# An encoder block on one core: the last mixer tile by column halves, the router spread over the tiles, rows stored unmodulated

## The chip, the core and the metric

The kernel runs on one NeuronCore of a Trainium2 chip. The metric is the device time of one execution in microseconds (us). The engines are TensorE (PE, matrix products and transposes), VectorE (DVE), ScalarE (ACT), GpSimd (POOL) and SyncE (SP, here only an issuer of transfers). Each engine works through its own list of instructions in order; lists meet through semaphores.

## What is computed

One layer of an encoder on 1024 positions of 1024 channels, in float32: a conditioning vector gives shifts, scales and gates; a mixer (Fourier branch and short convolution, gated) adds to the residual; then 16 experts with expert choice, and a last norm. The part around the change:

```python
x = x + gate_m[:, None, :] * mix_out              # mix_out = z @ w_o

h2 = modulate(rms_norm(x, g_norm_moe[l]), shift_f, scale_f)   # h*(1+scale)+shift
# expert_choice_moe(h2):
probs = softmax(h2 @ w_router + b_router)          # 16 experts
vals, idx = top_k(probs of each expert over positions, 128)
a = xe @ w_gate_e ; u = xe @ w_up_e                # xe: the 128 rows chosen
y = (silu(a) * u) @ w_down_e * vals
x = x + gate_f[:, None, :] * scatter_add(y at idx)
return rms_norm(x, g_final)
```

Products are made in three passes: each operand is split into a high part (rounded) and a low part (the rest), and high x high, high x low and low x high are summed.

## The kernel before

A planner of the language orders each engine's instructions when the kernel is built: what stands earlier in the program goes first, as soon as the planner believes its inputs and buffers ready. `tc.issue_after(ins)` holds instructions back behind another one. So a pool's number of buffers also moves the order.

*Mixer output, `mix_out` (L726).* Eight tiles t of 128 positions. A tile makes z @ w_o as 48 matmuls into one two-bank PSUM tile, for each k both column halves (`mm3`, L99). Then DVE adds the halves to x (L814, tile `ld`), ACT squares and sums them (L819), POOL makes the reciprocal root (`rstd`, L658), and DVE modulates the row in four pieces (L828, L830) into `h`, which POOL's queue stores to `h2_d` (L831); x itself goes to `x2_d` (L821). Modulation needs two rows broadcast to all partitions, loaded at t = 0. The router of tile t-1 stands at k = 6 of tile t: eight transposes with their split (`turn`, L731), 16 small matmuls against router weights that hold the modulation (`logits`, L743), softmax, and then `compare` (L848) for experts 0 and 1. Tile 7 has nobody behind it: its turning, router and the ranking of tiles 6 and 7 follow its last matmul.

*Ranking.* Experts 0 and 1 are ranked by counting, tile after tile (`compare`: how many earlier values are at least as large, by a matmul against ones; the own tile's row by a transpose), so that expert 0 can be picked right behind tile 7. The other experts are ranked by a bisection in small steps (`router`, L894), handed out between the weight blocks of the first experts through `side`.

*Picking, `pick` (L961).* A one-hot over the place, matmuls against position and probability, an index, and an indirect gather of 128 normed rows from `h2_d` into `xg` on POOL's queue. `turn` (L994) transposes them in two halves into PSUM and splits them into `xh` and `xl`.

*Experts, `expert` (L1048).* The weights come as 24 units of 1 MB per expert through a ring of slots, issued by SP in the order of use (`fetch`, L1006), 15 slots in three pools (7 + 5 + 3). `unit` (L1023) splits a unit in two halves: ACT writes the rounded part (`whi`, L92 in `split`), DVE the rest (`wlo`, L93); each has 3 buffers. A half feeds six matmuls. For each quarter fc of the 2048 hidden channels there are a gate block (`a`), an up block (`u`), and down blocks into `y`, which lag one quarter. Before the last down block of expert e the rows of expert e+1 are turned. Behind it DVE weighs y by probability and gate (`ys`, L1126), and POOL adds it into `x2_d` by an indirect transfer (L1127). In the last expert the finished rows of `x2_d` come back as four extra units in the weight stream (places in `FIN`), are normed by `final` (L1159: two sums of squares and a scaling on ACT, a product on DVE, one on POOL) and stored; the last expert's own 128 rows follow.

## Time and profile before

| | |
|---|---|
| median of 3 runs | 1964.37 us (1959.64 to 1964.53) |
| profiled execution | 1961.4 us, span 1959.6 us |
| PE busy | 1881.2 us (96%), 8677 matmuls and transposes |
| VectorE busy | 1608.2 us (82%) |
| ScalarE busy | 1169.2 us (60%) |
| mean granted PE clock | 0.984 |
| moved by DMA | 549.03 MB, mean 280 GB/s |
| chain that ended last | PE 79%, DVE 10%, issue 6%, ACT 2% |

The mixer output begins near 640 us, the experts near 783 us, and the last expert's matmuls end near 1947 us. Busy shares are means over stages with different limits. Matmuls are pipelined and their ends are modelled, so a full PE may still hold short gaps. In a row of the chain or of a timeline the first two numbers are start and duration in us, and the bracket gives the idle time before the instruction and who ended it. The granted clock is given as a share of full speed.

### The profile page before, as it was taken

Reading aid. Unit: us, or ns where it says so; the run is one execution under the profiler, and the core shown is the slowest. Engines: PE = TensorE matmul, PEld = TensorE weight load, DVE = VectorE, ACT = ScalarE, POOL = GpSimd, SP = SyncE. Lnnn points to the kernel's source line nnn. Section 1 sums busy time; section 2 is a strip of 40 time slices with the busy share of each in tenths; the row PEclk is TensorE's granted clock in tenths of the full one; section 3 lists DMA queues with packets and bytes.
Section 4 is the critical chain, followed back from the end, with each engine's and each line's share of the span. In section 5 each row is a group of like instructions: output and inputs, shape, how many; then the busy total and the mean of one; then the engine's idle time right before and its main releaser. Section 6 shows DMA issues by size and latency. Waiting matters only on the chain.

```text
span 1959.6 us, 24141 instructions
## 1 busy us (share of the span) xinstructions
PE 1881.2 (96%) x8677; PEld 1505.6 (77%) x8677; DVE 1608.2 (82%) x2083; ACT 1169.2 (60%) x1402; POOL 141.7 (7%) x127
## 2 busy tenths in 40 slices
PE   6999999999999996999999999999999999999985
PEld 5788888777788874777888888777777877777764
DVE  5976669676753777999999999899999899998985
ACT  5533233433411422777777777777777777777784
POOL 1000000000131111000000000000000000000011
PEclk9999999999999997999999999999999999999997
DMA  8322224464764945999999999999999999999981
GB/s 296 128 65 65 86 86 151 160 223 171 258 240 121 328 148 208 361 327 375 373 369 384 376 370 356 384 363 356 387 359 360 381 365 361 381 369 350 378 309 79
DMA packets 245261, 549.03 MB, mean 280 GB/s; under 512 B 12644, under 2 KB 51652, under 8 KB 245140
## 3 DMA queue, kind: packets, MB, share of 16 engines
q1 hardware_dynamic: 230160, 496.07, 70.0%
q0 software_dynamic: 14128, 51.18, 8.2%
q8 instruction: 68, 1.11, 0.2%
q14 instruction: 53, 0.43, 0.1%
q10 hardware_dynamic: 852, 0.24, 0.1%
HBM read 507.61 MB, written 39.86 MB: 279 GB/s over the span
## 4 chain that ended last, share of the span: by engine, by line
PE 79%; DVE 10%; issue 6%; ACT 2%; DMA 1%; POOL 1%; POOLq 0%; SPq 0%; ACTq 0%; DVEq 0%
PE pb L314 9%; PE u L1157 6%; PE pa L314 6%; DVE wlo L93 6%; PE pc L314 6%; PE u L1155 6%; PE u L1156 6%; PE a L1157 5%; PE a L1156 4%; PE a L1155 4%; PE y L105 4%; PE y L108 4%; PE y L111 4%; PE mm L111 3%; PE mm L105 3%
## 5 line engine op out<-in xcount | busy, mean ns | idle before, releaser
L93 DVE TENSOR_TENSOR wlo<-raw,whi 128x1024 fp32r<-128x1024 f32 x765 | 912.1, 1225 | 64.9 <-ACT whi L92 52.4
L92 ACT ACTIVATE whi<-raw 128x1024 fp32r<-128x1024 f32 x765 | 803.1, 1060 | 216.0 <-PE y L111 78.1
L1157 PE MATMUL a<-wlo,xh 128*128 128x512 f32 x512 | 208.5, 407 | 10.3 <-DVE wlo L93 9.5
L1155 PE MATMUL a<-whi,xh 128*128 128x512 f32 x512 | 204.4, 399 | 6.8 <-ACT whi L92 6.8
L1157 PE MATMUL u<-wlo,xh 128*128 128x512 f32 x512 | 204.7, 400 | 2.4 <-DVE wlo L93 1.8
L1155 PE MATMUL u<-whi,xh 128*128 128x512 f32 x512 | 204.3, 399 | 0.2 <-ACT whi L92 0.2
L1156 PE MATMUL a<-whi,xl 128*128 128x512 f32 x512 | 203.4, 397 | 0.2 <-DVE xl L93 0.2
L1156 PE MATMUL u<-whi,xl 128*128 128x512 f32 x512 | 202.7, 396 | 0.0
L108 PE MATMUL y<-wlo,hth 128*128 128x512 f32 x508 | 162.6, 401 | 2.6 <-DVE wlo L93 2.6
L105 PE MATMUL y<-whi,hth 128*128 128x512 f32 x508 | 160.8, 397 | 2.4 <-ACT whi L92 2.4
L111 PE MATMUL y<-whi,htl 128*128 128x512 f32 x508 | 158.6, 393 | 0.0
L1157 PEld LDWEIGHTS a<-wlo,xh 128*128 128x128 f32 x512 | 97.0, 190 | 44.5 <-DVE wlo L93 23.3
L92 ACT ACTIVATE wh<-s 128x512 fp32r<-128x512 f32 x80 | 50.3, 631 | 134.9 <-PE pc L314 73.4
L1157 PEld LDWEIGHTS u<-wlo,xh 128*128 128x128 f32 x512 | 96.7, 189 | 28.9 <-DVE wlo L93 6.1
L1155 PEld LDWEIGHTS a<-whi,xh 128*128 128x128 f32 x512 | 97.5, 190 | 27.1 <-ACT whi L92 7.2
L1156 PEld LDWEIGHTS a<-whi,xl 128*128 128x128 f32 x512 | 97.4, 190 | 23.4 <-DVE xl L93 0.7
L1156 PEld LDWEIGHTS u<-whi,xl 128*128 128x128 f32 x512 | 96.7, 189 | 21.9
L1155 PEld LDWEIGHTS u<-whi,xh 128*128 128x128 f32 x512 | 96.8, 189 | 21.0 <-ACT whi L92 0.6
L111 PEld LDWEIGHTS y<-whi,htl 128*128 128x128 f32 x508 | 95.8, 189 | 21.0
L105 PEld LDWEIGHTS y<-whi,hth 128*128 128x128 f32 x508 | 93.8, 189 | 22.0 <-ACT whi L92 2.9
L108 PEld LDWEIGHTS y<-wlo,hth 128*128 128x128 f32 x508 | 92.0, 189 | 22.0 <-DVE wlo L93 4.5
L92 ACT ACTIVATE wh<-ld 128x512 fp32r<-128x512 f32 x68 | 42.4, 629 | 88.1 <-issue 36.1
(523 smaller groups left out, 3157.2 us busy)
## 6 DMA issues: line engine op xcount, KB each, us to landing
raw<-in_w_gate_e_dram SPq DMA_DIRECT2D x128, 1024.0 KB, 8.4
raw<-in_w_up_e_dram SPq DMA_DIRECT2D x126, 1024.0 KB, 7.6
raw<-in_w_down_e_dram SPq DMA_DIRECT2D x126, 1024.0 KB, 8.2
ld<-in_w_ada_dram SPq DMA_DIRECT2D x48, 512.0 KB, 5.0
ld<-in_w_in_dram SPq DMA_DIRECT2D x44, 512.0 KB, 4.6
sg_d<-q POOLq DMA_DIRECT2D x8, 1024.0 KB, 5.0
ld<-sg_d SPq DMA_DIRECT2D x16, 512.0 KB, 4.3
x<-in_x_dram SPq DMA_DIRECT2D x8, 512.0 KB, 5.1
```

Source lines behind the costliest of these rows:

```text
L92: self.nc.scalar.activation(hi, src, AF.Copy)
L93: self.nc.vector.tensor_tensor(lo, src, hi, op=OP.subtract)
L105: nc.tensor.matmul(o, lhsT=lh, rhs=rh, start=first, stop=False)
L108: nc.tensor.matmul(o, lhsT=lh, rhs=rl, start=False, stop=False)
L111: nc.tensor.matmul(o, lhsT=ll, rhs=rh, start=False, stop=last)
L314: nc.tensor.matmul(o, lhsT=x[:, k, :], rhs=y[:, k, :], start=first and k == 0 and i == 0, stop=last and k == 3 and i == 2, skip_group_chec ...
L1155: nc.tensor.matmul(o, lhsT=lhs[0], rhs=rhs[0], start=first, stop=False)
L1156: nc.tensor.matmul(o, lhsT=lhs[1], rhs=rhs[0], start=False, stop=False)
L1157: nc.tensor.matmul(o, lhsT=lhs[0], rhs=rhs[1], start=False, stop=last)
```

## The change

It has five parts, all in the second half of the kernel.

1. Tile 7 is made by column halves: first all k for columns 0 to 511, then for 512 to 1023. Add, square sum, turning and router matmuls of the first half run while the second half is made.
2. The router of the tile before is spread: the ranking of the tile before that at k = 0, turning at k = 2, router matmuls and softmax at k = 4 (in tile 7 at k = 0, 4 of the first and 0 of the second half). `compare` takes both experts together, in two parts around a `yield`, makes the own row first, copies it on ACT, and counts ties with one more compare over the own tile. The softmax is made on negated logits, which saves the subtraction of the maximum.
3. Rows are stored normed but unmodulated, one ACT copy with the row's factor in place of four DVE pieces, and in tile 7 on SP's queue, ahead of the store of x. The modulation is made in the experts' `turn`, where channels lie on partitions: for expert 0 four ACT and four DVE pieces of 128x128 per half, for the others four ACT pieces per half into an f32 buffer `xf`, a copy and a subtraction. The column vectors `vc` stay in memory for it.
4. The weighing of y and its scatter-add are put off behind the first weight unit of the next expert (`self.left`, run in `up`); the load of the final gain follows them.
5. The ring shrinks from 7 + 5 + 3 to 7 + 4 + 1 slots, the split buffers grow from 3 to 6 of each part. How many halves are split ahead of the first gather (`NWS` in `unit`) stays 3.

```diff
-NRA, NRB, NRC, NWO = 7, 5, 3, 6
-NWS = 3
+NRA, NRB, NRC, NWO = 7, 4, 1, 6
+NWS, NWB = 3, 6
...
+        def turn(x2, xt, hf):
+
+            xth, xtl, pt = xt
+            hs = slice(4 * hf, 4 * hf + 4)
+            for k in range(4 * hf, 4 * hf + 4):
+                nc.tensor.transpose(pt[:, k, :], x2[:, k * P:(k + 1) * P], self.ident)
+            self.split(xth[:, hs, :], xtl[:, hs, :], pt[:, hs, :])
...
+        def softmax(t, rs, pl):
...
+            nc.vector.tensor_reduce(mn, lg, axis=AX.X, op=OP.min)
             se = pool.tile([P, 1], F32, name="se", bufs=2)
-            nc.scalar.activation(lg, lg, AF.Exp, accum_out=se)
+            nc.scalar.activation(lg, lg, AF.Exp, scale=-1.0, bias=mn, accum_out=se)
             nc.vector.reciprocal(se, se)
             nc.vector.tensor_scalar(self.prob[:, t, :], lg, se, None, op0=OP.mult)
...
+        def psum():
+            return self.pss.tile([P, 512], F32, name="sm")
+
+        def add_x(x2, ps, i):
+            cs = slice(512 * i, 512 * i + 512)
+            nc.vector.tensor_tensor(x2[:, cs], ps[:, cs], x2[:, cs], op=OP.add)
+
+        def sumsq(x2, h2, ss, i):
+            cs = slice(512 * i, 512 * i + 512)
+            nc.scalar.activation(h2[:, cs], x2[:, cs], AF.Square, accum_out=ss[:, i:i + 1])
+
+        def norm(x2, h2, ss, ts, eng):
+            nc.vector.tensor_tensor(ss[:, 0:1], ss[:, 0:1], ss[:, 1:2], op=OP.add)
+            rs = self.rstd(pool, ss[:, 0:1], "y")
+            nc.scalar.activation(h2, x2, AF.Copy, scale=rs)
+            eng.dma_start(out=self.h2_d[ts, :], in_=h2)
+            self.afterld = eng.dma_start(out=self.x2_d[ts, :], in_=x2).ins
+            return rs
+
+        def side(n):
+
+            if prev is None:
+                return
+            t, x2, rs = prev
+            if n == 0 and t:
+                for _ in self.compare(t - 1, range(NCMP), psum):
+                    pass
+            if n == 2:
+                hold["xt"] = turned()
+                for hf in range(2):
+                    turn(x2, hold["xt"], hf)
+            if n == 4:
+                pl = psum()
+                for hf in range(2):
+                    logits(pl, hold["xt"], hf)
+                softmax(t, rs, pl)
+
+        prev, hold = None, {}
...
+            if t < ST - 1:
+                for k in range(KD):
+                    side(k)
+                    self.mm3([ps[:, 0:512], ps[:, 512:1024]], (zh[:, k, :], zl[:, k, :]),
+                             [(self.wo[0][:, k, n:n + 512], self.wo[1][:, k, n:n + 512]) for n in (0, 512)],
+                             first=(k == 0), last=(k == KD - 1))
+                for i in range(2):
+                    add_x(x2, ps, i)
+                for i in range(2):
+                    sumsq(x2, h2, ss, i)
+                prev = (t, x2, norm(x2, h2, ss, ts, nc.gpsimd))
+                continue
+            xt = None
+            for n in range(2):
+                cs = slice(512 * n, 512 * n + 512)
+                for k in range(KD):
+                    if n == 0 and k % 2 == 0:
+                        side(k // 2)
+                    if n == 1 and k == 0:
+                        side(4)
+                    if n == 1 and k == 3:
+                        xt = turned()
+                        turn(x2, xt, 0)
+                    if n == 1 and k == 5:
+                        cmp = self.compare(t - 1, range(NCMP), psum)
+                        next(cmp)
+                    if n == 1 and k == 7:
+                        pl = psum()
+                        logits(pl, xt, 0)
+                    self.mm3([ps[:, cs]], (zh[:, k, :], zl[:, k, :]), [(self.wo[0][:, k, cs], self.wo[1][:, k, cs])],
+                             first=(k == 0), last=(k == KD - 1))
+                add_x(x2, ps, n)
+                if n == 0:
+                    sumsq(x2, h2, ss, n)
+            next(cmp, None)
+            turn(x2, xt, 1)
+            sumsq(x2, h2, ss, 1)
+            rs = norm(x2, h2, ss, ts, nc.sync)
+            logits(pl, xt, 1)
+            softmax(t, rs, pl)
...
+        for i in range(ne):
+            nc.tensor.transpose(row[:, i, :], p[i].to_broadcast([P, P]), self.ident)
+        if not last:
+            nc.scalar.activation(self.prow[:, e0:e0 + ne, n:n + P], row, AF.Copy)
+        ms = []
+        for i, e in enumerate(es):
+            w = n if last else n + P
+            m = pool.tile([P, (ST - 1) * P], BF16, name="cmp", bufs=2)
+            nc.vector.tensor_scalar(m[:, 0:w], self.prow[:, e, 0:w], p[i], 0.0, op0=OP.is_ge, op1=OP.add,
+                                    accum_out=cnt[:, 0, i:i + 1])
+            ms.append(m)
+        for i, e in enumerate(es):
+            own = pool.tile([P, P], BF16, name="own", bufs=2)
+            r = row[:, i, :] if last else self.prow[:, e, n:n + P]
+            nc.vector.scalar_tensor_tensor(own, in0=r, scalar=p[i], in1=self.upper, op0=OP.is_equal, op1=OP.mult,
+                                           accum_out=cnt[:, 1, i:i + 1])
+            if last:
+                own = pool.tile([P, P], BF16, name="own", bufs=2)
+                nc.vector.tensor_scalar(own, r, p[i], 0.0, op0=OP.is_ge, op1=OP.add, accum_out=cnt[:, 2, i:i + 1])
+        yield
+        for i in range(ne):
+            for j in range(t):
+                nc.tensor.matmul(num[:, i, j:j + 1], lhsT=ms[i][:, j * P:(j + 1) * P], rhs=self.onesb[:, 0:1],
+                                 start=True, stop=True)
...
+            nc.vector.tensor_tensor(place[:, :, 0:t], place[:, :, 0:t], num[:, :, 0:t], op=OP.subtract)
+        own = place[:, :, t]
+        if last:
+            nc.vector.tensor_tensor(cnt[:, 0, :], cnt[:, 0, :], cnt[:, 2, :], op=OP.add)
+        nc.vector.tensor_tensor(cnt[:, 0, :], cnt[:, 0, :], cnt[:, 1, :], op=OP.subtract)
+        self.after = nc.vector.tensor_tensor(own, own, cnt[:, 0, :], op=OP.add).ins
...
-        nc.vector.tensor_tensor(oh, self.pos[:, :, e:e + 1].to_broadcast([P, ST, P]),
+        pos = self.place[:, e, :, None] if e < NCMP else self.pos[:, :, e:e + 1]
...
+    def turn(self, pool, idx, val, xg, first=False):
...
+            hs = slice(4 * hf, 4 * hf + 4)
+            f = pool.tile([P, 4, P], F32, name="xf")
+            for k in range(4):
+                a, b = (self.vc[:, j + 4 * hf + k:j + 4 * hf + k + 1] for j in (16, 0))
+                if first:
+                    nc.scalar.activation(xh[:, 4 * hf + k, :], pt[:, k, :], AF.Identity, scale=a, bias=b)
+                    nc.vector.tensor_scalar(f[:, k, :], pt[:, k, :], a, b, op0=OP.mult, op1=OP.add)
+                else:
+                    nc.scalar.activation(f[:, k, :], pt[:, k, :], AF.Identity, scale=a, bias=b)
+            if not first:
+                nc.scalar.activation(xh[:, hs, :], f, AF.Copy)
+            nc.vector.tensor_tensor(xl[:, hs, :], f, xh[:, hs, :], op=OP.subtract)
...
                         self.mm3x(ps, (xh[:, k, :], xl[:, k, :]), (wh[:, i, :], wl[:, i, :]), k == 0, k == KD - 1)
                         k += 1
+                if self.left:
+                    self.left.pop()()
...
+            if last and fc == 0:
+                self.gl = pool.tile([P, D], F32, name="ys")
+                nc.gpsimd.dma_start(out=self.gl, in_=self.io["g_final"].rearrange("(o d) -> o d", o=1)
+                                    .partition_broadcast(P))
...
         if not last:
             down(3, 1)
-            ys = pool.tile([P, D], F32, name="ys")
-            nc.vector.scalar_tensor_tensor(ys, in0=y, scalar=val, in1=self.gf, op0=OP.mult, op1=OP.mult)
-            nc.gpsimd.indirect_dma_start(out=self.x2_d, out_offset=bass.IndirectOffsetOnAxis(ap=idx[:, 0:1], axis=0),
-                                         in_=ys, in_offset=None, compute_op=OP.add)
-            self.scattered = e == NE - 2
+
+            def add():
+                ys = pool.tile([P, D], F32, name="ys")
+                nc.vector.scalar_tensor_tensor(ys, in0=y, scalar=val, in1=self.gf, op0=OP.mult, op1=OP.mult)
+                nc.gpsimd.indirect_dma_start(out=self.x2_d,
+                                             out_offset=bass.IndirectOffsetOnAxis(ap=idx[:, 0:1], axis=0),
+                                             in_=ys, in_offset=None, compute_op=OP.add)
+                self.scattered = e == NE - 2
+
+            self.left.append(add)
...
-        gwsp, self.wsp = pool("mwsp", "right", bufs=NWS)
+        gwsp, self.wsp = pool("mwsp", "right", bufs=NWB)
...
+        picked = self.turn(mp, *picked, first=True)
+        self.left = []
```

## Rows read from the trace of the kernel before

**Rows 1.** Busy time by stretch (columns first): handover, middle experts, last expert.

```profile
core 0: us, PE busy (x) PEld busy (x) DVE busy (x) ACT busy (x) POOL busy (x), PEclk, DMA share, GB/s
700.00:740.00 40.00, 39.57 (x224) 31.77 (x223) 28.82 (x109) 9.34 (x21) 3.87 (x7) 1.00 0.24 92
...
760.00:780.00 20.00, 5.59 (x46) 4.83 (x46) 15.64 (x59) 2.20 (x4) 4.97 (x6) 0.50 0.82 307
...
1004.86:1074.90 70.04, 69.86 (x322) 56.61 (x321) 65.91 (x64) 55.31 (x58) 3.87 (x2) 1.00 1.03 375
1357.22:1428.61 71.39, 70.55 (x322) 56.23 (x320) 64.66 (x64) 55.05 (x59) 3.62 (x3) 1.00 1.01 367
1900.00:1930.00 30.00, 19.87 (x71) 14.59 (x70) 20.52 (x19) 22.07 (x29) 9.20 (x6) 0.77 0.30 120
```

**Rows 2.** Chain that ended last, from the last mixer tile on: start, us, what.

```profile
753.79 0.70 DVE ld L814
...
755.92 0.69 DVE htl L93
...
767.90 6.65 DMA h_d<-h
...
775.59 4.95 DMA xg<-h_d,idx
...
783.70 0.80 PE a L1156
```

**Rows 3.** Timeline of DVE, router and pick of the last tile.

```profile
765.11 0.23 DVE L752 SCALAR_TENSOR_TENSOR lg<-sm,yrs,rb 128x16 f32<-128x16 f32 x1 [1.91 <-PE sm L749]
...
768.59 1.15 DVE L859 TENSOR_SCALAR_CACHE_REDUCE cmp<-prow,prob 128x896 bf16<-128x896 f32 x1
...
771.84 1.22 DVE L968 TENSOR_TENSOR oh<-pos,slot 128x1024 bf16<-128x1024 f32 x1
...
773.72 0.16 DVE L981 SCALAR_TENSOR_TENSOR idx<-r 128x1 int32<-128x1 f32 x1
```

**Rows 4.** Timeline of PE: first and last of tile 7's 16 router matmuls.

```profile
761.51 0.37 PE L747 MATMUL sm<-wr,hth 128*128 128x32 f32 x1
...
764.71 0.36 PE L749 MATMUL sm<-wr,htl 128*128 128x16 f32 x1
```

**Rows 5.** Groups by line and shape, 640 to 785 us.

```profile
L830 DVE TENSOR_TENSOR h<-h,sf 128x512 f32<-128x512 f32 x16 | 10.9, 684 | 0.0
...
L92 ACT ACTIVATE zh<-ya 128x128 fp32r<-128x128 f32 x4 | 1.0, 298 | 5.0 <-DVE ya L610 5.0
L93 DVE TENSOR_TENSOR zl<-ya,zh 128x128 fp32r<-128x128 f32 x4 | 1.0, 278 | 0.0
```

**Rows 6.** Groups of ACT, whole run: eviction without and with scale and shift.

```profile
L92 ACT ACTIVATE hth<-tp 128x512 fp32r<-128x512 f32 x64 | 37.5, 586 | 8.9 <-PE tp L1077 8.2
...
L218 ACT ACTIVATE hg<-sm,shift,scale 128x512 f32<-128x512 f32 x4 | 3.0, 772 | 4.3 <-PE sm L142 4.3
```

**Rows 7.** Tile xg: its 17 gathers, issue to landing.

```profile
DMA to landing us min/median/max: 3.4/7.9/9.7
```

**Rows 8.** Timeline of POOL: two of 15 scatter-adds, seven experts apart.

```profile
1285.91 2.32 POOL L1127 DMA_INDIRECT x_d<-ys,idx  x1 [48.98 <-DVE ys L1126]
...
1785.31 2.32 POOL L1127 DMA_INDIRECT x_d<-ys,idx  x1 [51.58 <-DVE ys L1126]
```

**Rows 9.** Timeline of PE just after an expert begins.

```profile
1786.22 0.51 PE L1157 MATMUL a<-wlo,xh 128*128 128x512 f32 x1 [0.66 <-DVE wlo L93]
```

**Rows 10.** Waits of PE, 740 to 1960 us: total, times, longest.

```profile
PE a L1157 <- DVE wlo L93: 9.5, 16, 1.4
```

**Rows 11.** Timeline of PE, last expert: first and last of five stops.

```profile
1910.56 0.79 PE L1155 MATMUL a<-whi,xh 128*128 128x512 f32 x1 [6.76 <-ACT whi L92]
...
1937.69 1.22 PE L108 MATMUL y<-wlo,hth 128*128 128x512 f32 x2 [1.84 <-DVE wlo L93]
```

**Rows 12.** Waits of SP, 780 to 1900 us: total, times, longest.

```profile
SPq L1018 <- DVE wlo L93: 876.9, 342, 24.8
```

More of the change, by code (lines that the diff above doesn't have):

```diff
@@ L801, in mix_out @@
             ps = self.psm.tile([P, D], F32, name="mm")
-            for k in range(KD):
-                if k == 6 and prev is not None:
-                    logits(t - 1, prev[1], *turn(prev[0]))
-                    for e in range(NCMP):
-                        self.compare(self.cmpp, lambda: self.pss.tile([P, 512], F32, name="sm"), t - 1, e)
-                self.mm3([ps[:, 0:512], ps[:, 512:1024]], (zh[:, k, :], zl[:, k, :]),
-                         [(self.wo[0][:, k, n:n + 512], self.wo[1][:, k, n:n + 512]) for n in (0, 512)],
-                         first=(k == 0), last=(k == KD - 1))
@@ L810, in mix_out @@
             h2 = pool.tile([P, D], F32, name="h2")
             ss = pool.tile([P, 2], F32, name="ss2", bufs=2)
-            for i in range(2):
-                cs = slice(512 * i, 512 * i + 512)
-                nc.vector.tensor_tensor(x2[:, cs], ps[:, cs], x2[:, cs], op=OP.add)
-            if t == ST - 1:
-                xt = turn(x2)
-            for i in range(2):
-                cs = slice(512 * i, 512 * i + 512)
-                nc.scalar.activation(h2[:, cs], x2[:, cs], AF.Square, accum_out=ss[:, i:i + 1])
@@ L841, in router_consts @@
         nc.vector.tensor_copy(self.v5[:, :, :, 0:2], tk[:, :, None, :].to_broadcast([P, ST, NE, 2]))
+        self.vc = pool.tile([P, 24], F32, name="vc")
         self.prow = pool.tile([P, NCMP, (ST - 1) * P], F32, name="prow")
@@ L846, in router_consts, with compare @@
                                     op0=OP.mult, op1=OP.add)
-    def compare(self, pool, psum, t, e):
+    def compare(self, t, es, psum):
         nc = self.nc
-        p = self.prob[:, t, e:e + 1]
-        place = self.place[:, e, :]
+        pool = self.cmpp
+        e0, ne = es[0], len(es)
+        place = self.place[:, e0:e0 + ne, :]
         n = t * P
-        cnt = pool.tile([P, 3], F32, name="cnt", bufs=2)
+        last = t == ST - 1
+        cnt = pool.tile([P, 3, ne], F32, name=f"cnt{ne}", bufs=2)
@@ L856, in compare @@
         pc = psum()
-        if t:
-            m = pool.tile([P, (ST - 1) * P], BF16, name="cmp", bufs=2)
-            nc.vector.tensor_scalar(m[:, 0:n], self.prow[:, e, 0:n], p, 0.0, op0=OP.is_ge, op1=OP.add,
-                                    accum_out=cnt[:, 0:1])
-            for i in range(t):
-                nc.tensor.matmul(pc[:, P + i:P + i + 1], lhsT=m[:, i * P:(i + 1) * P], rhs=self.onesb[:, 0:1],
-                                 start=True, stop=True)
-        nc.tensor.transpose(pc[:, 0:P], p.to_broadcast([P, P]), self.ident)
@@ L865, in compare @@
-        if t < ST - 1:
-            row = self.prow[:, e, n:n + P]
-            nc.vector.tensor_copy(row, pc[:, 0:P])
-        else:
-            row = pc[:, 0:P]
-        own = pool.tile([P, P], BF16, name="own", bufs=2)
-        nc.vector.scalar_tensor_tensor(own, in0=row, scalar=p, in1=self.low, op0=OP.is_equal, op1=OP.mult,
-                                       accum_out=cnt[:, 1:2])
-        nc.vector.tensor_scalar(own, row, p, 0.0, op0=OP.is_gt, op1=OP.add, accum_out=cnt[:, 2:3])
-        if t:
-            nc.vector.tensor_tensor(place[:, 0:t], place[:, 0:t], pc[:, P:P + t], op=OP.subtract)
-            nc.vector.tensor_tensor(place[:, t:t + 1], place[:, t:t + 1], cnt[:, 0:1], op=OP.add)
@@ L877, in compare @@
-        nc.vector.tensor_tensor(place[:, t:t + 1], place[:, t:t + 1], cnt[:, 1:2], op=OP.add)
-        last = nc.vector.tensor_tensor(place[:, t:t + 1], place[:, t:t + 1], cnt[:, 2:3], op=OP.add)
-        if t == ST - 1:
-            self.after = last.ins
-            nc.vector.tensor_copy(self.pos[:, :, e], place)
+        row = pc[:, 0:ne * P].rearrange("p (e s) -> p e s", e=ne)
+        num = pc[:, 256:256 + 8 * ne].rearrange("p (e t) -> p e t", e=ne)
+        p = [self.prob[:, t, e:e + 1] for e in es]
@@ L956, in route_rest @@
     def route_rest(self, pool):
-        self.compare(self.cmpp, self.psum, ST - 1, 1)
+        yield from self.compare(ST - 1, (1,), self.psum)
         self.ranked = NCMP
@@ L1283, in run @@
         nc.gpsimd.dma_start(out=self.trib, in_=self.seg("tri"))
-        for n in ("slot", "tok", "low"):
+        for n in ("slot", "tok", "upper"):
             a, b = SEG[n]
@@ L1312, in psum @@
             return self.ptp.tile([P, 512], F32, name="tp")
-        self.compare(p, psum, ST - 1, 0)
+        for _ in self.compare(ST - 1, (0,), psum):
+            pass
         with tc.issue_after(self.after):
```

106 lines of the change are left out of this document (36 added, 70 removed).

## The prediction

> **What bounds the kernel now.** I read the busy time by stretch first, then the chain that ended last through the handover from mixer to experts, then the timelines of single engines where that chain stops, and last the waits.
>
> By stretch, TensorE (PE) is the bound almost everywhere: 39.57 of 40.00 us busy while mixer tiles run, 69.86 of 70.04 us in an expert [rows 1]. VectorE stands right behind it in an expert (65.91 us), ScalarE has room (55.31 us). The DMA share of 1.0 looks like a second bound, but SP, which issues the weight loads, spent 876.9 us in 342 waits for the split that frees a ring slot [rows 12]: the loads wait for the engines. So three places are left where PE loses time.
>
> The handover: between 760 and 780 us PE is busy 5.59 of 20 us, at half clock [rows 1]. The chain [rows 2] starts with the add of the last mixer tile at 753.79, goes through router, ranking, the storing of the normed rows (landed 6.65 us after 767.90) and the gather (4.95 us from 775.59), and reaches the second matmul of expert 0 at 783.70: 29.9 us.
>
> The expert boundary: a period is 70.04 us in a good expert and 71.39 us in most later ones [rows 1]; seven of the latter take 499.4 us, 71.34 each [rows 8]. Right behind the boundary PE waits for a low part of a weight split on VectorE [rows 9], 16 times, 9.5 us [rows 10]; the y weighing and the two row splits are queued there among the weight splits.
>
> The last expert: PE stops five times, 6.76, 1.36, 1.84, 2.44 and 1.84 us, 14.2 in all, the first and the last of them in [rows 11], for splits queued behind the final norm of rows. From 1900 to 1930 its clock is 0.77 [rows 1], so by that share some 3 to 5 us more (an estimate) go to the lower of its two levels.
>
> **The change part by part.**
>
> *Handover.* From the end of the last matmul of tile 7, the new chain is: add of one half and its turning. Before, add to second split piece took 755.92 + 0.69 - 753.79 = 2.8 us [rows 2]; I keep it. Router matmuls of one half only, the other half having run inside the tile: 16 took 764.71 - 761.51 + 0.4 = 3.6 us [rows 4], so 8 take 1.8. Softmax: 768.59 - 765.11 = 3.5 us [rows 3], of which three modulation pieces of 0.68 to 0.74 us [rows 5] stood in between; without them 1.4. Ranking against the earlier tiles: 771.84 - 768.59 = 3.25 [rows 3]; the wide compare (1.15) and both own-tile counts stay, the transposed row now comes first and the copy of the places goes: 2.7. One-hot, matmuls, index: 773.72 + 0.16 - 771.84 = 2.0. Issue of the gather 0.5. Its landing was 4.95 us, the median of all 17 is 7.9, the slowest 9.7 [rows 7]; now it falls into the four weight loads issued just before it, so I take 6.4, between the first two. Turning of expert 0's rows to its matmul: 783.70 - 775.59 - 4.95 = 3.2, plus four pieces of 0.278 [rows 5] on VectorE for the modulation: 4.3. Sum 2.8 + 1.8 + 1.4 + 2.7 + 2.0 + 0.5 + 6.4 + 4.3 = 21.9 against 29.9, 8.0 less. The storing of the normed rows is off the chain: sum of squares, power and one copy on ScalarE (twice 0.586 us [rows 6]) put its issue some 4 us after the add, and with the 6.65 us of before it lands at 11, about when the index is ready (11.2); were it 3 us later, all 3 would be lost. To be paid: tile 7 now holds eight router matmuls (0.9 warm), the rest of tile 6's, four transposes and its ranking, about 2 us of PE ahead of the end; the earlier tiles can return at most the 0.43 us of idle per 40 us [rows 1], 1 us. Handover: 7 us gained, bounds 3 (slowest gather) and 10.
>
> *Spreading the router steps over a tile* costs and gives nothing else: PE runs the same matmuls and was busy. VectorE drops the modulation, four pieces of 0.7 us per tile; ScalarE gets one copy of 1.2 us per tile, covered by its idle time (9.34 of 40 us busy [rows 1]). Fewer loads at tile 0 are hidden by the stream.
>
> *Expert boundary.* The weighing of y moves behind the first weight unit of the next expert, and the split buffers grow from 3 to 6 pairs. One pair feeds PE for 69.86 / 48 = 1.46 us, so PE has 4.4 us more in hand. If every period became the good one, seven give 1.3 each, 9; with the boundaries before and behind them I put it at 11. Against it stands the modulation in each turn. ScalarE evicts 128x512 in 0.586 us, with scale and shift in 0.772 [rows 6], 0.19 more; a 128x128 piece takes 0.298 [rows 5], so with both about 0.48. Eight of these and two copies are 5.0 us where 1.2 were, 3.9 more in each of 15 turns. ScalarE's total goes to 59 of 70 us, which it has; the added time in the turn must be covered by split pairs in hand. I take 8 us gained, bounds 14 gained (also the short waits of good boundaries gone) and 15 lost (1 us at each boundary).
>
> The Trainium skill (ScalarE: Activation LUTs, Rules for kernel authors) speaks against this part: multiplies and adds belong on VectorE. Its figures (same page, What ACT_TABLE_LOAD costs) put a 128-column piece with two pointer operands at 0.48 us, overlapping by 0.09; by that the turn costs 3.1 us more, not 3.9, and the sum stays. On the rule itself the row decides otherwise: VectorE is 94% busy in an expert and ScalarE 79% [rows 1], so the eight pieces would hurt more there.
>
> *Last expert.* The stops come where ScalarE is in the final norms of rows, two of them in a row, and the splits behind them wait. Three more pairs hide 4.4 us of the first stop; the later ones find the buffers refilled only in part. 5 us gained, bounds 0 (norms drawn together differently) and 14.
>
> *Ring of 12 slots, not 15.* 12 MB at 375 GB/s [rows 1] are 33 us of stream; loads wait for slots today, so nothing. Cover gone would mean splits waiting for loads, which no wait shows now. *Scatter-add one unit (2 x 1.46 = 2.9 us) later:* POOL waits for it anyway; behind it only the load of the final gain and the reload of rows in the last expert, which are used near its end. Nothing.
>
> Sum: 7 + 8 + 5 = 20. The profiled execution took 1961.4 us (span 1959.6), so 1941.4; the median of the runs shown is 3.0 above it, so 1944 in its terms.
>
> **The rivals.**
>
> *Everything hides.* The deeper buffers take the boundaries to their best (14) and most of the last expert (12), handover 9: 35 gained, 1929. For it: all waits behind the boundary name one queue. Against: VectorE has only 4 us per expert to run ahead with.
>
> *Only the handover.* The longer turn takes back what the buffers give, the norms stay: 7 to 9 gained, 1956. For it: with one f32 buffer for the modulated half, the second half of a turn waits for VectorE's subtraction of the first.
>
> *Slower: the turn becomes the new wait at each boundary.* Place: that f32 buffer. Chain: four pieces 1.9, copy 0.6, subtraction 0.7, twice, is 6.4 us, and PE's cover from the transposes to the second half's first use is four pairs, 5.8 us. If one weight split stands ahead on each engine in each half (1.1 and 1.2 us), the chain is 11 and PE stops 5.2 us 15 times: 78 lost less the 1.4 of today each, 57 net, less 12 from the other parts: 2009. It decides against the change from 12 / 15 = 0.8 us of stop beyond today's. Against: the turn's pieces come earlier in the program than the splits they'd wait for, and rows are gathered long ahead. By the rule of the Trainium skill given above (ScalarE: Activation LUTs, Rules for kernel authors) this would be the outcome of putting the pieces on ScalarE. Its 21% of idle time in an expert [rows 1] speaks against it.
>
> *The spread does nothing.* That PE was 99% busy through the tiles makes this nearly certain for tiles 0 to 6, and it is in the sum.
>
> **How the numbers follow.** Forecast 0.55, everything hides 0.17, only the handover 0.18, slower 0.10, most of this near the point of decision (1960 to 1985). The range 1926 to 1963 holds the first three with their bounds and leaves out the far ends. A measurement of this kernel tells 0.3% (6 us) from no change. Faster by more: 0.55 + 0.17 + 0.12 of the third and a little of the rest, 0.85; within it 0.08; slower 0.07.
>
> **What would show it.** Right: the first expert matmul about 21 us behind the last mixer add; the store of normed rows landed before the gather's index; 15 even periods below 70.8 us, no wait of PE for a low part behind a boundary; in the last expert the first stop near 2 us. Wrong: PE waiting for a row split (xh or xl) after each turn; splits waiting for weight loads; the gather waiting for the store; stops in the last expert as long as before.

## The result and the profile after

The changed kernel took 1991.94 us (median of 4 runs, 1990.36 to 1997.72) against 1963.5 of the kernel before in the same comparison: ratio 1.0154, 95% interval 1.0128 to 1.0179. It is slower by 28 us, where I had forecast 20 faster.

By stretch (the changed kernel; span, busy time per engine, granted clock):

```profile
640.00:660.00 20.00, 17.16 (x82) 13.68 (x82) 14.23 (x25) 8.52 (x18) 2.22 (x4) 1.00 0.82 272
...
785.00:795.00 10.00, 7.16 (x28) 5.11 (x27) 8.14 (x26) 4.10 (x8) 0.00 (x0) 0.57 0.67 258
1012.58:1084.06 71.48, 70.52 (x322) 56.48 (x321) 65.94 (x64) 57.88 (x68) 3.89 (x3) 1.00 1.01 367
1446.90:1520.21 73.31, 71.53 (x320) 56.12 (x320) 64.10 (x64) 54.26 (x67) 3.63 (x3) 1.00 1.00 359
```

The last two lines are an early and a late expert, like the two in [rows 1]: where an early one took 70.04 it takes 71.48, and where a late one took 71.39 it takes 73.31, with full clock and VectorE and ScalarE no busier than 92%. The other two lines are new losses, at the start of the mixer tiles and behind the handover.

Between the start of the first mixer-output matmul, the last one, the first gate matmul of expert 1, that of expert 15 and the end of the span, the two profiled executions differ like this (from the trace's start times, us):

| stretch | before | after | difference |
|---|---|---|---|
| eight mixer tiles | 113.5 | 121.9 | +8.3 |
| last mixer matmul to expert 1 | 105.0 | 102.9 | -2.1 |
| experts 1 to 14 | 995.7 | 1017.7 | +22.1 |
| expert 15 and the end | 105.6 | 105.9 | +0.4 |

So the experts lost 22, a mean of 1.58 in each of 14 periods: 5.4 in experts 2 to 5, 17.0 in experts 6 to 14, while expert 1 gave 0.3 back. The handover gained too little to pay for the tiles. With 0.2 from before the tiles the sum is, within rounding, the 29.0 between the spans 1959.6 and 1988.6.

**The late boundary** (the ten into experts 6 to 15). ScalarE between two late experts of the changed kernel:

```profile
1433.86 0.60 ACT L92 ACTIVATE hth<-tp 128x512 fp32r<-128x512 f32 x1 [1.60 <-PE tp L1151]
1434.35 2.00 ACT L92 ACTIVATE whi<-raw 128x1024 fp32r<-128x1024 f32 x2
1438.47 1.51 ACT L1072 ACTIVATE xf<-tp,vc 128x128 f32<-128x128 f32 x4 [2.12 <-PE tp L1063]
1439.86 1.07 ACT L92 ACTIVATE whi<-raw 128x1024 fp32r<-128x1024 f32 x1
1440.81 0.64 ACT L1074 ACTIVATE xh<-xf 128x512 fp32r<-128x512 f32 x1
...
1444.60 1.09 ACT L92 ACTIVATE whi<-raw 128x1024 fp32r<-128x1024 f32 x1
```

VectorE and PE there:

```profile
1436.17 2.35 DVE L93 TENSOR_TENSOR wlo<-raw,whi 128x1024 fp32r<-128x1024 f32 x2
1440.96 1.23 DVE L93 TENSOR_TENSOR wlo<-raw,whi 128x1024 fp32r<-128x1024 f32 x1 [2.44 <-ACT whi L92]
...
1445.34 1.28 DVE L1202 SCALAR_TENSOR_TENSOR ys<-y,val,gf 128x1024 f32<-128x1024 f32 x1 [0.28 <-PE y L111]
1446.54 1.22 DVE L93 TENSOR_TENSOR wlo<-raw,whi 128x1024 fp32r<-128x1024 f32 x1
```

```profile
1442.24 0.74 PE L108 MATMUL y<-wlo,hth 128*128 128x512 f32 x2 [0.53 <-DVE wlo L93]
1447.81 0.50 PE L1236 MATMUL a<-wlo,xh 128*128 128x512 f32 x1 [1.03 <-DVE wlo L93]
```

ScalarE splits two halves, and then its next instruction is the first modulation piece, whose transposes PE has not made yet. It sits idle for 2.12 us with buffers free, then does 1.51 us of pieces before the next split. VectorE starves for 2.44 us, and PE comes to the missing low part at 1442.24. The second stop (1.03 at 1447.81) ends with the low part of 1446.54. Its high part was ready at 1445.69, behind the second four pieces. By then VectorE stood at the weighing of y (part 4), which waited 0.28 for PE and ran until 1446.62. So both the pieces and the weighing stand ahead of that split, and no run separates what each costs here.

**The early boundary** (the four into experts 2 to 5) is another case. There ScalarE does not stop for the transposes. The second half's pieces wait for VectorE to empty the one f32 buffer `xf`, and PE waits for the rows' low part `xl`. Waits between 800 and 1900 us (who waited for whom, us in total, times, longest):

```profile
PE a L1235 <- DVE xl L1075: 2.7, 4, 0.9
ACT xf L1072 <- DVE xl L1075: 2.0, 4, 0.7
```

**The tiles.** In tile 1 PE sums the router weights' products; a row of PE's timeline, and one of VectorE's with what that sum waits for:

```profile
658.37 1.93 PE L786 MATMUL sm<-wsf,ones 128*128 128x16 f32 x16 [2.76 <-DVE wsf L779]
```

```profile
657.64 0.18 DVE L775 COPY vc<-sm 128x24 f32<-128x24 f32 x1 [2.87 <-DMA z_d<-ya]
```

The first write of the channel vectors `vc` waits for a store of `ya`, a block of the merge stage that has nothing to do with them. Tile 1 took 20.3 us where it had taken 13.4, and the clock granted between 660 and 680 was 0.91.

**The handover**, in the chain of waits:

```profile
762.99 0.61 DVE ld L795
...
773.15 0.67 issue
773.81 8.49 DMA xg<-h_d,idx
782.44 1.10 PE tp L1063 x4
...
789.46 0.80 PE a L1235
```

From the add to the second matmul it is 26.5 us against 29.9 [rows 2].

### The profile page after: what moved, and what is told of

It reads as the page before. It is cut to its first block, busy times and chain, and to the rows that moved or that the text cites. A ratio compares the mean times of both kernels' runs of the same rounds, so it can differ in the third digit from the quotient of the medians.

```text
span 1988.6 us, 23938 instructions
## 1 busy us (share of the span) xinstructions
PE 1897.5 (95%) x8677; PEld 1505.4 (76%) x8677; DVE 1575.3 (79%) x1978; ACT 1184.8 (60%) x1543; POOL 144.3 (7%) x124
## 4 chain that ended last, share of the span: by engine, by line
PE 79%; DVE 9%; issue 4%; DMA 4%; ACT 3%; POOL 1%; ACTq 0%; POOLq 0%; DVEq 0%
PE pb L314 8%; PE pa L314 6%; PE pc L314 6%; PE u L1236 5%; PE y L108 5%; DVE wlo L93 5%; PE y L105 5%; PE u L1235 5%; PE y L111 5%; PE u L1234 5%; PE a L1236 4%; PE a L1235 4%; PE a L1234 4%; PE mm L105 3%; PE mm L108 3%
## 5 line engine op out<-in xcount | busy, mean ns | idle before, releaser
L92 ACT ACTIVATE whi<-raw 128x1024 fp32r<-128x1024 f32 x765 | 768.9, 1058 | 77.1 <-PE y L111 31.7
L108 PEld LDWEIGHTS y<-wlo,hth 128*128 128x128 f32 x508 | 92.1, 190 | 29.9 <-DVE wlo L93 11.9
```

Of the source, the lines that this page charges most:

```text
L92: self.nc.scalar.activation(hi, src, AF.Copy)
L108: nc.tensor.matmul(o, lhsT=lh, rhs=rl, start=False, stop=False)
```

## The experiments

All ratios are against the kernel before, run on the same chip in the same comparison (median 1961 to 1963). Late periods are those of experts 7 to 13, early ones those of experts 2 to 4, both from the trace's start times. The code ahead of the mixer output is the same everywhere, yet the first mixer-output matmul starts between 639.5 and 646.3 us in the profiled executions; so a few us between medians of few runs say less than a stretch of the traces. The views of waits below are of PE between 1300 and 1800 us, which is seven late boundaries: engine, line, what ended the wait, us in total, times, longest. The changed kernel has there:

```profile
PE a L1236 <- DVE wlo L93: 7.2, 7, 1.0
PE y L108 <- DVE wlo L93: 3.2, 6, 0.5
```

**1. Part 5 undone.**

```diff
-NRA, NRB, NRC, NWO = 7, 4, 1, 6
-NWS, NWB = 3, 6
+NRA, NRB, NRC, NWO = 7, 5, 3, 6
+NWS, NWB = 3, 3
```

> The changed kernel with part 5 undone (ring 7+5+3, three split buffers of each part). Theory T (the eight modulation pieces of a turn hold up ScalarE's list at each boundary): the buffers are not the cause, the time stays within 6 us of the changed kernel, 1986 to 1998. Theory S (the six split buffers and the short ring make the matmuls' pitch or the order of the lists worse): 12 to 20 us come back, 1972 to 1980, and the period of an expert falls by about 1 us.

2003.5 us, ratio 1.0206 (1.017 to 1.0243): some 11 us worse, outside both theories. Periods from expert 9 on stay at 73.26, early ones go from 71.47 to 72.85 and expert 1 from 73.5 to 77.9. The six buffers are not the cause of the loss; the kernel is worse without them, in its earlier experts above all.

**2. Part 3 undone** (rows modulated by VectorE in the tiles and stored so; `turn` only splits).

```diff
-            nc.scalar.activation(h2, x2, AF.Copy, scale=rs)
+            for i in range(2):
+                cs = slice(512 * i, 512 * i + 512)
+                nc.vector.scalar_tensor_tensor(h2[:, cs], in0=x2[:, cs], scalar=rs, in1=a2[:, cs],
+                                               op0=OP.mult, op1=OP.mult)
+                nc.vector.tensor_tensor(h2[:, cs], h2[:, cs], sf[:, cs], op=OP.add)
```

> The changed kernel with part 3 undone: rows stored modulated (four VectorE pieces per tile instead of one copy), the experts' turns split only. Theory T: periods fall from 73.2 to about 71.5, some 24 us come back less up to 2 us for the longer handover chain, 1966 to 1972. Theory S: the periods stay at 73 and the time stays above 1984.

1966.42 us, ratio 1.0016 (1.0003 to 1.0029). 25.5 us come back; late periods 71.38, early 69.99. ScalarE waits just as long for the transposes, but has one piece of 0.6 behind the wait:

```profile
1424.97 0.60 ACT L92 ACTIVATE xh<-tp 128x512 fp32r<-128x512 f32 x1 [2.13 <-PE tp L1075]
1425.47 2.00 ACT L92 ACTIVATE whi<-raw 128x1024 fp32r<-128x1024 f32 x2
```

PE's waits there:

```profile
PE a L1237 <- DVE wlo L93: 2.8, 7, 0.4
```

Experts 1 to 14 take 997.0 us: 20.8 of the 22.1 lost there come back. The modulation in the turn is the loss.

**3. Part 5 alone, on the kernel before.** The numbers of the first diff the other way round.

> The kernel before with part 5 alone (ring 7+4+1, six split buffers of each part). Theory T: 1955 to 1966, no slower than before, by my prediction 5 to 10 us faster. Theory S: 10 to 20 us slower than before, 1973 to 1984, with a longer period in every expert.

1962.19 us, ratio 0.9991 (0.9977 to 1.0005): nothing that the medians could tell. What ScalarE waits for shows why, before (first view) and with six buffers (second), same stretch:

```profile
ACT whi L92 <- PE y L111: 30.5, 77, 0.7
ACT whi L92 <- PE a L1156: 24.8, 56, 1.3
ACT whi L92 <- PE u L1156: 16.4, 42, 0.7
```

```profile
ACT hth L92 <- PE tp L1077: 64.7, 28, 4.5
ACT h L1102 <- PE a L1157: 58.4, 28, 3.1
ACT xh L92 <- PE tp L1002: 16.1, 14, 2.1
```

With three buffers ScalarE waits for a free one (71.7 us here). With six it waits in its list instead (139 us), at the activation `h`, the split of its transposes and the row split, which need PE's latest results. PE's wait for the low part is the same in both:

```profile
PE a L1157 <- DVE wlo L93: 4.6, 7, 0.7
```

At late boundaries, then, the lead is set by where those three stand in the list once the buffers suffice. Early periods do shrink, from 70.05 to 69.52, and expert 1's from 73.8 to 72.6.

**4. Part 4 alone, on the kernel before.**

```diff
+                if self.left:
+                    self.left.pop()()
...
+            self.left.append(add)
```

> The kernel before with part 4 alone (weighing of y and its scatter-add behind the first weight unit of the next expert). By theories T and S alike the first waits for a low part behind a boundary (9.5 us in 16 times) get shorter: 1955 to 1964. Were the weighing in its new place the cause (theory L: it stands in VectorE's list among the first splits of the expert), it would be 10 us or more slower, above 1974.

1960.51 us, ratio 0.9987 (0.9976 to 0.9999): 2 us or so gained, theory L falls. Late periods go from 71.3 to 71.1. That is the weighing without the pieces; what it costs or gives beside them was not tried.

**5. Two f32 buffers** (`name="xf", bufs=2`).

> The changed kernel with two f32 buffers for the modulated half instead of one. Theory F (the rival of my prediction: the second half's pieces wait until VectorE has subtracted the first half): the wait goes, 10 us or more come back, below 1982. Theory T2 (ScalarE's list holds only two weight splits between the last block it waited for and the modulation pieces, so when it stops for the transposes PE has some three pairs in hand, and the 3.1 us of added ScalarE work behind that wait are not covered): the buffer was never waited for, 1986 to 1998.

2004.32 us, ratio 1.0224 (1.0207 to 1.0241): 12 us worse, above both theories' ranges. Late periods rise to 74.2. Freed from the buffer, the eight pieces stand closer together in the list and starve PE three times per late boundary:

```profile
PE y L108 <- DVE wlo L93: 10.8, 21, 0.5
PE y L105 <- ACT whi L92: 2.8, 7, 0.4
```

At late boundaries the buffer was not what was waited for. At early ones it was: early periods fall from 71.47 to 70.49, and between 940 and 1155 us, where PE had waited 2.7 us for `xl`, it now waits

```profile
PE a L1235 <- DVE xl L1075: 0.7, 3, 0.2
```

Expert 1 takes that gain back (78.2 in place of 73.5).

**6. Four more splits ahead of the pieces.** The two halves of the last down block and two of the next expert's are split earlier in the program, and the turn is held behind them.

```diff
+            w = list(self.unit(2))
+            self.pre.append(list(self.unit(4)))
+            with self.tc.issue_after(self.whi):
+                nxt = self.turn(pool, *nxt)
+            down(3, 1, w)
```

> The changed kernel with the same work in another order: the splits of the last down block and of the next expert's first unit stand ahead of the modulation pieces in ScalarE's list (six in place of two behind the last turned h block). Theory T2: the six buffers are now full when ScalarE stops for the transposes, the stops of 0.9 us in the last down block and of 1.4 us at 2.6 us into the next expert go, late periods fall from 73.25 to 71.0 to 71.8: 1965 to 1977. Theory W (the added ScalarE and VectorE work itself, wherever it stands, makes the period longer): nothing comes back, 1986 or more.

2012.43 us, ratio 1.0255 (1.0236 to 1.0274). The two waits for low parts of weights went as expected, but the rows are late now, and the mean granted clock fell from 0.983 to 0.973:

```profile
PE a L1238 <- DVE xl L1075: 20.2, 7, 2.9
```

Late periods are 75.1. I had looked at one side of the list only. And the place in the list is not alone here: the second half's pieces stop for the one f32 buffer, 2.2 us at each boundary:

```profile
ACT xf L1072 <- DVE xl L1075: 15.3, 7, 2.2
```

Four more splits ahead with two f32 buffers was not tried.

**7. Pieces on VectorE.**

```diff
-                    nc.scalar.activation(f[:, k, :], pt[:, k, :], AF.Identity, scale=a, bias=b)
+                    nc.vector.tensor_scalar(f[:, k, :], pt[:, k, :], a, b, op0=OP.mult, op1=OP.add)
```

> The changed kernel with the experts' modulation pieces on VectorE in place of ScalarE (eight of 128x128 per expert, about 0.3 to 0.4 us each), the rounding copy stays on ScalarE. Rule R (multiplies and adds belong on VectorE): ScalarE gets back 3 us behind its wait, 10 us or more come back, below 1982. Theory T2: the chain behind the transposes only changes engine, and VectorE, the busier one (64 of 73 us), rebuilds its lead more slowly: 1985 to 2010, with the early periods (router on VectorE beside it) the worst.

1993.95 us, ratio 1.0163 (1.0145 to 1.0181): no better, as theory T2 had it. Late periods fall by 0.7 to 72.5, expert 1, with the router beside it, rises from 73.5 to 77.2. PE's waits are smaller and more (9.8 us in 21 times):

```profile
PE a L1236 <- DVE wlo L93: 9.8, 21, 0.7
```

**8. Rows modulated, router weights prepared at tile 0** (`if t == 0:` ahead of `router_weights()`).

> The changed kernel with rows stored modulated (as in the run before) and the router's weights prepared at tile 0 instead of tile 1. Theory M (the sum of the router weights' products waits on PE for VectorE, whose list has the add of tile 0 ahead of it: 3 us of stop in tile 1, and the lower clock behind it): tiles 0 and 1 together take 26 to 29 us in place of 31.8, 1960 to 1964. If the stop comes from the loads of those weights instead, it stays: 1965 to 1968.

1968.52 us, ratio 1.0034 (1.0016 to 1.0051). Theory M falls: PE's stop in tile 1 stays (2.56 us), and VectorE's copy into `vc` waits for the same store, 3.13 us. That points at the memory, not the place in the program.

**9. The channel vectors in the pool of constants.**

```diff
-        self.vc = pool.tile([P, 24], F32, name="vc")
+        self.vc = self.cpool.tile([P, 24], F32, name="vc")
```

> The changed kernel with one tile moved: the channel vectors are kept in the pool of constants, which is free from the start, in place of the pool that opens in the memory of the merge stage. Theory P (the vectors' tile lies where a block of the merge stage lay, and its first write waits 2.9 us for that block's store to land, with the weights of the router and PE behind it): the stop of 3.2 us in tile 1 goes, tile 1 falls from 20.3 to 15 to 17 us, 1984 to 1989. If the stop has another cause: 1990 to 1996.

1989.52 us, ratio 1.0134 (1.0119 to 1.0148). Tile 1 takes 15.8 in place of 20.3, and the copy no longer waits:

```profile
657.79 0.18 DVE L775 COPY vc<-sm 128x24 f32<-128x24 f32 x1
```

Theory P holds by the trace; of the 4.6 us in the tile the medians show 2.4, which leaves the time half a us above its range.

**10. As 9, two more splits ahead** (without the `pre` line of 6).

> The run above with two more splits ahead of the modulation pieces in ScalarE's list (four in place of two, where six made a stop of 3.3 us for the low part of the rows). Theory T3 (between the transposes and the next expert there is no place for the pieces that suits both sides: ahead of the splits they starve PE, behind them the rows are late): a stop on each side, each shorter, late periods 71.8 to 73.0 against 73.25, so 3 to 15 us less than the run above. If the order were all, the periods would reach the 71.4 of the kernel with modulated rows, 18 us less.

1975.46 us, ratio 1.0065 (1.0051 to 1.008): 14 us less than 9, late periods 71.8. ScalarE now comes to the transposes as they are made:

```profile
1429.79 3.90 ACT L1111 ACTIVATE whi<-raw 128x1024 fp32r<-128x1024 f32 x4
1433.92 1.51 ACT L1072 ACTIVATE xf<-tp,vc 128x128 f32<-128x128 f32 x4 [0.23 <-PE tp L1063]
```

and PE stops a little on each side:

```profile
PE y L108 <- DVE wlo L1112: 3.3, 7, 0.5
...
PE a L1237 <- DVE xl L1075: 1.5, 6, 0.3
```

With 0, 2 and 4 more splits ahead the late periods are 73.25, 71.8 and 75.1: the same work at three places in one list. The third also pays the wait for the f32 buffer (run 6); in run 10 that wait is 0.5 us per boundary. 71.38 is what rows modulated in the tiles give.

**11. As 10, expert 0's rows turned like the others'** (`first=True` left out).

> The changed kernel with constants pool and two more splits ahead, and expert 0's rows turned like the others' (pieces on ScalarE into the f32 buffer, copy, subtraction) instead of pieces on both engines. From the first transposes to the second matmul of expert 0 it was 7.0 us there, where I had 4.3 for this stretch. Theory Q (the pieces of both engines on one PSUM block go one after the other, eight in a row per half): four pieces of 0.4, a copy of 0.6 and a subtraction of 0.7 are 2.9 us and the stretch falls to 4.5 to 5.5 us, 1 to 3 us less than 1975.5. If what stands between them in VectorE's list (weight splits) is the cause, it stays at 6.5 to 7.5.

1972.1 us, ratio 1.0052 (1.0035 to 1.0068). From the first transposes (783.32) to the second matmul (787.79) it is 4.5 us, and expert 0's period falls from 80.7 to 76.0. With pieces on both engines they had gone in turns (ScalarE in the changed kernel):

```profile
783.56 0.46 ACT L1069 ACTIVATE xh<-tp,vc 128x128 fp32r<-128x128 f32 x1 [9.77 <-PE tp L1063]
784.50 0.46 ACT L1069 ACTIVATE xh<-tp,vc 128x128 fp32r<-128x128 f32 x1 [0.48 <-DVE xf L1070]
...
790.04 0.46 ACT L1069 ACTIVATE xh<-tp,vc 128x128 fp32r<-128x128 f32 x1 [2.10 <-DVE xf L1070]
```

ScalarE's pieces wait for VectorE's. VectorE itself doesn't stop between 784.06 and 789.41, the end of `xl`: weight splits of 1.2 us stand between its pieces, and PE waits for the last of these.

```profile
784.45 1.21 DVE L93 TENSOR_TENSOR wlo<-raw,whi 128x1024 fp32r<-128x1024 f32 x1
785.58 0.40 DVE L1070 TENSOR_SCALAR xf<-tp,vc 128x128 f32<-128x128 f32 x1
785.90 1.21 DVE L93 TENSOR_TENSOR wlo<-raw,whi 128x1024 fp32r<-128x1024 f32 x1
787.03 0.41 DVE L1070 TENSOR_SCALAR xf<-tp,vc 128x128 f32<-128x128 f32 x1
```

```profile
788.66 0.47 PE L912 MATMUL tp<-ident,prob 128*128 128x128 f32 x1 [2.51 <-DVE xf L1070]
```

So theory Q has the number but not the whole mechanism. Run 11 takes VectorE's pieces away altogether, so it can't tell the turns of the two engines from the splits between VectorE's pieces; the trace points at the splits.

**12. Rows modulated and `vc` in the mixer's pool** (run 2, with `vc` allocated where the kernel before has it).

> The changed kernel with part 3 undone whole: rows stored modulated, and the channel vectors back in the mixer's pool. Theory P: the stop in tile 1 goes here too, 4 to 6 us less than 1966.4, so 1960 to 1963; parts 1, 2, 4 and 5 together are then worth 0 to 3 us. If it stays: 1965 to 1968.

1956.78 us, ratio 0.9968 (0.9958 to 0.9979), 9.6 us less than run 2, below the range of theory P, and a little faster than both kernels (0.3% below the one before). Tile 1 gives 4.5 of it. The rest came unexpected, see the last section.

**13. Run 12 with two more splits ahead.**

> The run above with two more splits ahead of the row splits in ScalarE's list. There the turn is short (0.6 and 0.7 us per half), so by theory T3 the later place costs nothing and the stop of 0.8 us at 3 us into each late period goes: late periods 70.4 to 71.0 in place of 71.4, 1952 to 1958, faster than both kernels. If those stops come from VectorE being full, the periods stay: 1959 to 1964.

1954.1 us, ratio 0.996 (0.9948 to 0.9972). The time lies in my range, but most of that is run 12's gain: late periods moved from 70.98 only to 70.87. The stop of 0.8 us at 3 us is another one, and my reason for it was wrong.

**14. Run 13 without column halves** (tile 7 like the others, then its turning, the ranking of tile 6, the router).

> The kernel with modulated rows and two more splits ahead (1954.1), with part 1 undone: tile 7 made like the others, its turning, its router and the ranking of tile 6 behind it. By my prediction's terms the chain from the last mixer matmul to the first transposes of expert 0's rows gets 4 to 6 us longer (it is 21.7 there) and tile 7 some 2 us shorter: 1956 to 1958. If column halves are worth nothing (the gather or the store of rows ends the chain): 1952 to 1955.

1950.17 us, ratio 0.994 (0.9923 to 0.9957), the lowest median, and below what either case expected. Tile 7 takes 14.7 in place of 16.8 us. From the last mixer matmul to the first transposes it is 22.4 in place of 21.7: the index is ready 1.9 us later, but the gather landed in 6.4 in place of 7.5 us. So halves gain 0.7 in the chain and cost 2.1 in the tile, in one profile each. The 2.5 us by which the medians differ beyond that lie within the spread of the runs (1949.13 to 1957.37 and 1952.13 to 1957.13). The profiled execution is the slowest of the four (1957.37). Its tile 2 took 21.0 us against 14.6 in run 13, with this stop and the lower clock behind it:

```profile
678.45 0.87 PE L736 MATMUL mm<-ident,ld 128*128 128x128 f32 x4 [1.89 <-DVE htl L93]
```

The other three executions took 1949.1 to 1950.9; whether they have the stop isn't shown.

**15. Run 13 with an unused tile of 64 bytes per partition** (`mp.tile([P, 16], F32, name="pad")`).

> The same kernel of 1954.1 with an unused tile of 64 bytes per partition at the head of the experts' pool, so that the experts' tiles lie 64 bytes further; nothing else. Theory A (the matmuls' pitch hangs on where these tiles lie: gate and up matmuls 233 ns apart in most kernels, 229.5 in the two where the channel vectors left their pool): one of the pitches moves by 2 ns or more, the periods by 0.3 to 0.8 us, the time by 4 to 12 us either way. If the pitch comes from the order of the lists, all pitches stay within 1 ns, 1951 to 1957.

1955.08 us, ratio 0.9968 (0.9957 to 0.998): no difference to 1954.1. Read in the last section.

## Why the prediction was wrong, by its own steps

**Handover: right up to the index, then not.** I had 11.2 us from the add to the start of the gather and it took 10.8; the store of normed rows was not waited for, and the sign I named, "the first expert matmul about 21 us behind the last mixer add", came true (784.07 - 762.99 = 21.1). The gather took 8.49 where I took 6.4 (my bound was 9.7). The failed step is the turning, "plus four pieces of 0.278 [rows 5] on VectorE for the modulation: 4.3": from the landing at 782.30 it took 7.2. I counted VectorE's four pieces as if nothing stood between them; two weight splits and router steps did, and ScalarE's pieces waited for VectorE's (run 11). Together 26.5 against 21.9. And I priced nothing behind the second matmul: after the 9.8 us wait for the gather PE went on at the lower of its two levels (0.57 granted between 785 and 795, where it had been 0.93), and expert 0's period rose from 75.6 to 80.8. With the turn repaired (run 11), or with modulated rows, the stretch from the last mixer matmul to expert 1 is 99.4 to 99.9 us, 5 to 6 less than before, against my 8.0 before payment (tile 7's extra work lies ahead of this stretch). Without the column halves it is 99.5 as well (run 14): they are not what gained it, and which part did isn't shown.

**Spreading the router steps "costs and gives nothing else": wrong by 4.6 us.** The step looked at engines and loads. "The column vectors `vc` stay in memory" also means that they lie elsewhere, and there a store had to land first (run 9). Tile 7's extra work, 2 by my estimate, was 2.7. The other 1.0 of the tiles' 8.3 is spread over them and stays open.

**Expert boundary: the step that decided.** I forecast 8 gained and 22 were lost, 17 of them at late boundaries. "The added time in the turn must be covered by split pairs in hand" was right; "PE has 4.4 us more in hand" was not. That was a sum over buffers, and buffers bound a lead only from above. With three, the buffers were the bound; with six, the list is, because `h`, `hth` and the row pieces need what PE has just made and stand a few splits apart (run 3). At the turn two splits lay ahead, as in the kernel before, and 3 us of ScalarE work were put behind a wait. My figure for that work, 3.9, was on the high side: two times 1.51 + 0.64 in place of 0.60 is 3.1. At early boundaries the splits in hand sufficed (PE waits for none there), but what PE came to next was the rows themselves, with the one f32 buffer between their halves; my sum had no term for that, though my rival did.

The rule of the Trainium skill that I weighed (ScalarE: Activation LUTs, Rules for kernel authors: multiplies and adds belong on VectorE) would have given the right sign, but not by its reason. With the pieces on VectorE late periods are 0.7 shorter, expert 1 is 3.7 longer, and the time is no better (run 7). The 21% of idle ScalarE time by which I set the rival aside said little, as that idle time lies in waits (between 1300 and 1800 us in the kernel before, 72 us for free buffers and 32 for PE's results).

**Last expert: 5 gained, measured none.** Its first stop fell from 6.76 to 5.83 [rows 11], where I had 4.4 hidden by three more pairs; the others stayed about as long, and the stretch took 105.9 us against 105.6. With six buffers alone (run 3) and with rows modulated (run 2) the first stop is 5.9 and 5.8 too, so it isn't the pieces: again more buffers did not mean that much more lead.

**Ring, moved scatter-add:** nothing for the ring, as said (run 3); the moved weighing gave 2 us alone (run 4). Splits waited for loads 1.9 us in all between 800 and 1900.

**The rivals.** "The turn becomes the new wait at each boundary" is what happened. Its place, the f32 buffer, was right at the four early boundaries and wrong at the ten late ones, where that buffer was not waited for (run 5). I argued against the rival that "the turn's pieces come earlier in the program than the splits they'd wait for". That was the harm at late boundaries: coming earlier, they kept the splits waiting. The measured 1.58 us per period lies past the 0.8 from which I said it decides. Its chance of 0.10 was too low: the rows of the kernel before could not show pieces waiting inside a list, so they were no ground for setting it aside.

## What to carry to other kernels

An in-order engine that feeds another one can run ahead only to the next instruction in its list that needs the other's result: before adding buffers, count what stands between those instructions. Work put right behind such a wait is paid by the consumer even on an engine that is idle a fifth of the time; put it where the engine arrives just as its input does, and measure both sides (0, 2 and 4 splits: 73.25, 71.8, 75.1 us). Read more than one boundary: the early ones here stop for another reason than the late ones. A tile that moves to another pool can take over a wait of whoever had that memory before (here a store, 2.87 us).

## What was not expected

Runs 2 and 12 have the same instructions in the same order on all five engines; they differ in where `vc` lies and so, by its size, in the addresses of the experts' tiles, 96 bytes lower. Beside tile 1, every expert from 1 to 14 got 0.4 to 0.7 us shorter, 6.6 together: from start to start, gate and up matmuls are 233.0 ns apart in run 2 and 229.5 in run 12 (mean of those without a stop, from the trace). Down matmuls are 228.5 in the kernel before and 232 to 234 in all kernels with the changed code. At 96 of them per expert some 4 ns are 0.4 us, an estimated 5 us over 14 experts. The changed code loses this in run 2 as well, where the pieces are gone. Parts 4 and 5 about make up for it: alone, by their traces, they took 2.9 and 1.8 us off experts 1 to 14 (runs 4 and 3). Moving the same tiles up by 64 bytes (run 15) moved gate and up by 1.1 ns one way (229.4 to 228.3) and down by 1.0 the other (232.9 to 233.9). That is half of the 2 ns that I had asked for, and the time did not move, so run 15 alone doesn't decide. Runs 2 and 12, with the same lists and 3.5 ns between them, speak for placement; by which rule stays open. At 192 gate and up matmuls per expert 3.5 ns are 0.7 us; by the medians run 12 got 5.1 us beyond tile 1 (9.6 - 4.5), more than parts 4 or 5 alone were worth.

That the six-buffer ring helped the changed kernel by 11 us (run 1) and the kernel before by nothing (run 3) was not foreseen either. The trace of run 1 shows one of the waits: in expert 1 PE stops for the one-hot of the next pick, a stop that the changed kernel doesn't have.

```profile
PE tp L1036 <- DVE oh L1029: 1.9, 1, 1.9
```

Runs 5 and 7, whose expert 1 is as long (78.2 and 77.2), have it too (2.8 and 1.5 us). Why the router's steps come late there was not tried.
